# NaN-ignoring maximum over rows: the last key pass of 25 narrow tiles waits for two key buffers at once

## The chip, the cores and the metric

The kernel runs on one core of a Trainium2 chip. Four queues do its work: SyncE (SP) issues the loads and stores, ScalarE (ACT), GpSimd (POOL) and VectorE (DVE) compute; TensorE is not used. Each engine takes its instructions in the order in which they were written, and the engines wait for each other by semaphores that instructions count up. The metric is the time of one execution on the device, in microseconds (us).

## What is computed

```
x: (32, 2048, 2048) float32, a tenth of it NaN
out = nanmax(x, axis=-1)          # (32, 2048) float32
```

65,536 rows of 2048 numbers (536.87 MB) are read once; the maximum of each row without its NaNs is written (0.26 MB). There is next to no reuse, and three passes over the data have to be made while it streams through.

## The kernel before

[...] ScalarE reads them as signed integers and makes a 16-bit *key* (Prelu with a scale of -1, a bias and a steep negative slope: numbers keep their order, NaN patterns go to the far end). A *write-back* then turns the key into the upper half of the float again (times -1, plus TOP), where a NaN has become a very negative number. VectorE reduces the floats by maximum. At the end `find` turns the maxima of rows with nothing but NaNs into NaN.

The rows are spread over 128 partitions and cut into 69 tiles (TILES, numbered from 0), each held by one of three rooms of SBUF. A tile is given as loads, chunks and reductions in units of Q = 512 elements per partition: for each chunk the sizes of the key passes and the sizes of the write-backs. A write-back given as a plain number is POOL's; `(n, w)` is ScalarE's, put off until w more key passes have been issued; `(n, -1)` is VectorE's. Tile 55 is

```
([28], [([8], [(2, 1), 6]), ([8], [8]), ([12], [(3, 1), 9])], [16, 12])
```

one load of 28 Q, chunks of 8, 8 and 12 Q (key passes of 4096, 4096 and 6144 elements); of the first chunk ScalarE writes back 2 Q after the next pass, POOL 6 Q; two reductions of 16 and 12 Q.

Tiles 1 to 35 are wide (32 Q) and keep their keys in place. From tile 38 on (PLAIN) the tiles are narrow, 28 Q and then smaller parts, and the keys go to one of three key buffers of 12 Q, taken in turn. A chunk is put behind the one before it if it still fits; otherwise the next buffer is opened, and the first key pass into it waits until all write-backs out of it are done. `kfree[k]` holds, for each engine, the last write-back out of buffer k; `freed` turns this into waits.

A room is free for a new load when VectorE has made the last reduction of its tile; so the load of tile n + 3 is issued by SP (L495) when VectorE ends tile n. 

The order of the work on each engine is the order of the program's text: for each key pass the pass itself (`act`, L299), then ScalarE's write-backs that are due (`write`, L299), POOL's (L309), then the reductions whose data is written (L316). `Order.needed` leaves out a wait that is implied by one made before on that engine. Of several waits of one instruction the last is attached to it, the others become instructions of their own ahead of it (`engine.wait_ge`, L183).

Where one reduction needs exactly one write-back of ScalarE and one of POOL, `joints` gives the two a *pair* semaphore of their own in place of the engines' counts; whoever waits for the pair waits for both. In `write`, each write-back is entered into `kfree` with the count that the engine's next ordinary instruction will have; in `freed` that count replaces the pair for ScalarE, if it has been given out by then (L408 and the lines after):

```
for back, then, e in uses:
    if back == "act" and order.count["act"] >= then:
        e = ("act", then)
    if back != "pool" or e[0] == "pool" or all(v < then for v in counts):
        deps.append(e)
```

The place of the change is where a buffer is opened (L515):

```
elif used + fresh.get(step, 0) > KEYS:
    key = (key + 1) % NKEYS
    used = 0
    ...
    kold = freed(key, (key + 1) % NKEYS) if number in EARLY and at + c == end else freed(key)
```

`fresh` is the size of a chunk at its first pass; `at + c == end` holds for the last pass of a tile.

Of the kernel before, what the change touches and what calls it, by code (L numbers as in the profile page):

```python
# [91 lines left out]

LANES = 14

EARLY = ()

# [102 lines left out]
def kernel(  # L201
# [91 lines left out]
    with tc.tile_critical() as section:  # L293
# [108 lines left out]
        def freed(*ks):  # L402

            uses = [(back, then, e) for k in ks for back, ((_, then), e) in kfree[k].items()]
            counts = [e[1] for _, _, e in uses if e[0] == "pool"]
            deps = []
# [5 lines that stand above are left out]
            return deps  # L412
# [50 lines left out]
        for number, (loads, chunks, reds) in enumerate(TILES):  # L463
# [44 lines left out]
            for step, c in enumerate(keys):  # L508
# [6 lines left out]
                elif used + fresh.get(step, 0) > KEYS:  # L515
# [3 lines left out]
                    assert all(q[2] != key for v in half.values() for q in v)  # L519
                    kold = freed(key, (key + 1) % NKEYS) if number in EARLY and at + c == end else freed(key)  # L520
                    kfree[key] = {}
# [120 lines left out]
```

## Time and profile before

| | before |
|---|---|
| median of 3 runs | 1252.22 us (1252.11 to 1252.24) |
| the profiled execution | 1252.06 us |
| its span in the profile | 1250.3 us |
| VectorE busy | 1164.8 us (93%) |
| ScalarE busy | 1151.3 us (92%) |
| POOL busy | 1060.2 us (85%) |
| DMA | 537.21 MB, mean 430 GB/s |

The span runs from the first instruction of the program to the end of the last; the execution's time has a little around it. In the rows, a line number such as L299 is that of the helper which records the operation, so most of ScalarE's work has one line, key passes and write-backs alike: `kt<-xt` or `xt<-xt` from uint16<-int16 is a key pass (`xt<-xt` because two of the three key buffers lie in the big tensor), int16<-uint16 is a write-back. A row of the timeline gives start, duration, engine, line, operation, names, shapes and count; in brackets stands how long the engine was idle before it and who ended that. Rows of neighbouring instructions without a break are merged, with their count behind the x. Two instructions of one engine that follow each other closely overlap a little in the records.

### The profile page before, as it was taken

To read this page: it belongs to the slowest core of one execution; us is meant where nothing else is said; L and a number is where in the kernel's file an instruction comes from. 1 tells how busy PE (TensorE), PEld (TensorE's weight loads), DVE (VectorE), ACT (ScalarE), POOL (GpSimd) and SP (SyncE) were. 2 spreads that over 40 slices of the span, in tenths; PEclk is the share of its full clock that TensorE was granted. 3 is DMA by queue.
4 is the path that set the end of the run, shared out by engine and by line. 5 is a ranking of instruction groups with operands and counts; after the bars stand their busy time and mean duration, and the time that the engine had idled before them with its cause. 6 is when DMAs were issued, how large, how long until landed. Compare 5 with 4: busy or idle time off the path is not lost.

```text
span 1250.3 us, 1057 instructions
## 1 busy us (share of the span) xinstructions
DVE 1164.8 (93%) x252; ACT 1151.3 (92%) x294; POOL 1060.2 (85%) x253
## 2 busy tenths in 40 slices
DVE  0799999999999999999999998988889989999999
ACT  3999999999999999999999999898888789999998
POOL 0888788887988888888899998977999887999988
DMA  9999999999999999999999999999999999999997
GB/s 411 428 436 436 436 436 436 436 437 434 436 436 432 432 432 428 434 430 434 434 431 438 433 439 440 433 427 431 440 428 440 426 439 431 431 430 428 432 427 309
DMA packets 17240, 537.21 MB, mean 430 GB/s; under 512 B 2640, under 2 KB 2640, under 8 KB 5712
## 3 DMA queue, kind: packets, MB, share of 16 engines
q1 hardware_dynamic: 17232, 537.14, 99.5%
q14 instruction: 8, 0.07, 0.0%
HBM read 536.87 MB, written 0.26 MB: 430 GB/s over the span
## 4 chain that ended last, share of the span: by engine, by line
DMA 38%; DVE 25%; ACT 23%; POOL 14%; issue 1%; SPq 0%; ACTq 0%
DMA xt<-in_x_dram 38%; DVE acc L316 24%; ACT xt L299 21%; POOL xt L309 14%; ACT kt L299 2%; SPq L495 0%; SPq L286 0%; DVE acc L323 0%; SPq L637 0%; ACTq L183 0%; SPq L293 0%
## 5 line engine op out<-in xcount | busy, mean ns | idle before, releaser
L316 DVE TENSOR_REDUCE acc<-xt 128x3 f32<-128x6144 f32 (+3 forms) x219 | 1114.6, 5135 | 64.2 <-POOL xt L309 56.7
L309 POOL TENSOR_SCALAR xt<-xt 128x3584 int16<-128x3584 uint16 (+9 forms) x204 | 926.3, 4541 | 162.8 <-ACT xt L299 152.9
L299 ACT ACTIVATE xt<-xt 128x6144 uint16<-128x6144 int16 (+12 forms) x236 | 1006.3, 4361 | 62.8 <-DMA xt<-in_x_dram 61.9
L309 POOL TENSOR_SCALAR xt<-kt 128x4096 int16<-128x4096 uint16 (+10 forms) x34 | 128.8, 3789 | 21.2 <-ACT kt L299 19.7
L299 ACT ACTIVATE kt<-xt 128x4096 uint16<-128x4096 int16 (+10 forms) x42 | 118.9, 2852 | 29.7 <-DMA xt<-in_x_dram 29.4
L316 DVE TENSOR_SCALAR xt<-xt 128x2560 int16<-128x2560 uint16 x32 | 52.6, 1644 | 19.0 <-ACT xt L299 19.0
L299 ACT ACTIVATE xt<-kt 128x1536 int16<-128x1536 uint16 (+6 forms) x14 | 29.6, 2112 | 0.2
L331 POOL TENSOR_SCALAR late<-acc 128x112 int32<-128x112 f32 (+1 forms) x5 | 2.8, 558 | 0.4
L299 ACT ACT_TABLE_LOAD x1 | 1.3, 1283 | 1.3 <-SPq L293 1.3
L345 POOL TENSOR_TENSOR acc<-acc,late 128x112 int32<-128x112 int32 (+1 forms) x5 | 2.0, 397 | 0.4
L351 POOL MEMSET scalars<- 128x1 f32 x1 | 0.1, 98 | 0.9 <-SPq L293 0.9
L623 POOL MEMSET const-float32-0.0<- 128x1 f32 x1 | 0.1, 98 | 0.2 <-issue 0.2
L299 ACT ACTIVATE scalars<-scalars 128x1 f32<-128x1 f32 x1 | 0.2, 203 | 0.0
L323 DVE SCALAR_TENSOR_TENSOR acc<-acc 128x7 f32<-128x7 f32 x1 | 0.2, 166 | 0.0
L623 POOL MEMSET const-bfloat16-1.0<- 128x1 bf16 x1 | 0.1, 101 | 0.0
L623 POOL MEMSET const-uint8-127<- 128x1 uint8 x1 | 0.1, 101 | 0.0
L623 POOL MEMSET const-float32-1.0<- 128x1 f32 x1 | 0.1, 98 | 0.0
## 6 DMA issues: line engine op xcount, KB each, us to landing
xt<-in_x_dram SPq DMA_DIRECT2D x20, 7168.0 KB, 23.3
xt<-in_x_dram SPq DMA_DIRECT2D x5, 2304.0 KB, 25.6
xt<-in_x_dram SPq DMA_DIRECT2D x2, 5632.0 KB, 19.6
xt<-in_x_dram SPq DMA_DIRECT2D x3, 3584.0 KB, 25.0
xt<-in_x_dram SPq DMA_DIRECT2D x2, 4352.0 KB, 17.3
xt<-in_x_dram SPq DMA_DIRECT2D x2, 4096.0 KB, 19.7
xt<-in_x_dram SPq DMA_DIRECT2D x1, 7680.0 KB, 24.2
xt<-in_x_dram SPq DMA_DIRECT2D x9, 768.0 KB, 25.3
```

The costliest lines, as they stand in the source:

```text
L299: lambda: nc.scalar.activation(**kw),
L309: lambda: nc.gpsimd.tensor_scalar(**kw),
L316: return order.add("dve", nc.vector, lambda: do(**kw), deps)
L323: lambda: engine.scalar_tensor_tensor(out=acc, in0=acc, scalar=0.0, in1=acc, op0=ALU.mult, op1=ALU.add),
L331: lambda: engine.tensor_scalar(out=none, in0=acc, scalar1=LEAST, scalar2=float(0x00400000), op0=ALU.is_lt, op1=ALU.mult,),
L345: lambda: engine.tensor_tensor(out=bits, in0=bits, in1=none, op=ALU.add),
L351: e_top = order.add("pool", nc.gpsimd, lambda: nc.gpsimd.memset(top, EDGE), [])
L623: nc = _bacc.Bacc("TRN2", target_bir_lowering=False, num_devices=1)
```

## The change

The tuple EARLY, empty before, names 25 tiles. In these, if the last key pass opens a buffer, it waits for the write-backs out of this buffer and out of the next one as well, which the next tile's first pass will open. A wait made there needn't be made again by that later pass, so ScalarE's queue holds 16 wait instructions fewer. Loads, passes, write-backs, reductions, their sizes and their order are the same.

```
-EARLY = ()
+EARLY = (38, 39, 40, 41, 42, 43, 44, 45, 46, 47, 48, 50, 51, 52, 53, 54, 55, 56, 62, 63, 64, 65, 66, 67, 68)
```

## The prediction

> **What bounds the kernel now.** I read the page first, then busy time by stretch, then the chain of waits backwards from the end, and last the timeline of the stretch where the chain leaves the DMA queue. The page:
>
> ```profile
> span 1250.3 us, 1057 instructions
> DVE 1164.8 (93%) x252; ACT 1151.3 (92%) x294; POOL 1060.2 (85%) x253
> q1 hardware_dynamic: 17232, 537.14, 99.5%
> xt<-in_x_dram SPq DMA_DIRECT2D x20, 7168.0 KB, 23.3
> ```
>
> The loads fill 99.5% of the DMA engines' time, so up to the last landing nothing in the middle can cost anything unless the queue runs dry. A full narrow load (7168 KB, 7.34 MB) needs 17.0 us at the page's mean of 430 GB/s and lands 23.3 us after its issue: it is issued some 6 us before its turn. That is the first cover. But the end does not have it. Busy time by stretch (us; VectorE, ScalarE, POOL):
>
> ```profile
> 860.00:960.00 100.00, 88.94 (x16) 85.22 (x24) 91.83 (x19) 1.00 1.00 432
> 1030.00:1074.00 44.00, 41.33 (x8) 42.08 (x13) 36.10 (x9) 1.00 1.00 432
> 1074.00:1167.00 93.00, 92.90 (x20) 88.67 (x29) 88.10 (x25) 1.00 1.00 431
> 1167.00:1248.00 81.00, 80.96 (x32) 77.53 (x57) 72.34 (x36) 1.00 0.94 394
> ```
>
> Up to 1030 every engine has some 10% of room. From 1074 VectorE has 0.1 us of room in 93, and none after. The chain of waits says the same from its other end (start, us, what; pieces from 1030 on):
>
> ```profile
> 1032.08 23.38 DMA xt<-in_x_dram
> ...
> 1098.11 5.92 POOL xt L309
> ...
> 1104.05 21.67 DVE acc L316 x4
> ...
> 1164.35 2.48 POOL xt L309
> ...
> 1166.85 80.96 DVE acc L316 x31
> ```
>
> The last 81 us are 31 reductions without a break, then the last fold of `acc` and its store. So two things bound the time: loads until about 1030, and from there VectorE, which never gets back what it loses. What delays VectorE before 1030 is free as long as the queue is covered; after 1030 it goes to the end almost whole.
>
> **The change part by part.** *Where it acts.* `freed(key, next)` is asked only where the last pass of a tile opens a new key buffer (L515). In tiles 38, 39, 42, 62, 66, 67 and 68 the last pass is put into the buffer already open, by the sizes in TILES: seven of the 25 are not touched. In tile 51 the next buffer's write-back isn't recorded yet when it is asked, so nothing is added there. Seventeen are left: 40, 41, 43 to 48, 50, 52 to 56, 63 to 65.
>
> *What it removes.* The first pass of the next tile waits for its load and, before, for the write-backs of its buffer by an instruction of its own (L183). These go: 16. The chain shows one such wait of ScalarE where it did lie on the path:
>
> ```profile
> 957.49 0.02 issue
> 957.51 0.02 ACTq L183
> 957.53 0.04 issue
> ```
>
> It costs 0.06 us there, between the end of POOL's work (before 957.49) and the start of the pass (957.57). The 16 removed ones stand ahead of a pass that waits for its load; the write-back came earlier, so they are over while ScalarE idles or still runs the pass before. I take 0; at 0.06 each the other end is 16 x 0.06 = 1.0 us gained.
>
> A rule speaks for more. The Trainium skill (Advanced Engine Details and Errata, Network/Comms) gives 50 to 100 ns for a sequencer's reading of a semaphore; by it 16 waits would be an estimated 0.8 to 1.6 us. The one row above agrees with its lower end.
>
> *What it adds, before 1030.* A pass of ScalarE now waits for the POOL write-back of the chunk before the one just written. The largest cases are tiles 45 and 46 (start, us, engine, shapes, idle before):
>
> ```profile
> 857.88 6.48 POOL L309 TENSOR_SCALAR xt<-xt 128x5632 int16<-128x5632 uint16 x1 [5.45 <-ACT xt L299]
> 861.85 3.59 ACT L299 ACTIVATE kt<-xt 128x4096 uint16<-128x4096 int16 x1
> 869.37 9.68 ACT L299 ACTIVATE xt<-xt 128x6144 uint16<-128x6144 int16 x2 [3.94 <-DMA xt<-in_x_dram]
> 874.78 7.06 POOL L309 TENSOR_SCALAR xt<-xt 128x6144 int16<-128x6144 uint16 x1 [0.74 <-ACT xt L299]
> 878.96 2.75 ACT L299 ACTIVATE kt<-xt 128x3072 uint16<-128x3072 int16 x1
> 951.51 13.02 DVE L316 TENSOR_REDUCE acc<-xt 128x3 f32<-128x6144 f32 x2 [1.59 <-POOL xt L309]
> ```
>
> Tile 45: the pass at 861.85 needs the write-back that ends at 857.88 + 6.48 = 864.36, so it starts 2.5 later; ScalarE then idles 3.94 for the next load, and the lag is gone. Tile 46: the pass at 878.96 waits for 874.78 + 7.06 = 881.84, 2.9 later. This lag reaches POOL and VectorE, about 1.9 us, and tile 48's own early wait takes it up once more; but VectorE idles again by 951.51 for a POOL pass that follows a later load, so it ends there. Tiles 41, 43, 44, 48, 50, 52, 53 and 54 have 0.1 to 1.0 us by the same sum, each hidden by ScalarE's idle time for loads, which is
>
> ```profile
> ACT kt L299 <- DMA xt<-in_x_dram: 26.1, 9, 5.0
> ```
>
> 26.1 us in nine waits between 835 and 1034 (total, times, longest). Two us off the six by which a load is issued ahead leaves the queue full. Sum before 1030: 0.
>
> *What it adds in tile 55.* Its three passes have 4096, 4096 and 6144 elements:
>
> ```profile
> 1021.61 3.62 ACT L299 ACTIVATE kt<-xt 128x4096 uint16<-128x4096 int16 x1 [1.28 <-DMA xt<-in_x_dram]
> 1025.31 3.63 POOL L309 TENSOR_SCALAR xt<-kt 128x3072 int16<-128x3072 uint16 x1 [1.53 <-ACT kt L299]
> 1028.64 1.33 ACT L299 ACTIVATE xt<-kt 128x1024 int16<-128x1024 uint16 x1
> 1029.02 4.76 POOL L309 TENSOR_SCALAR xt<-xt 128x4096 int16<-128x4096 uint16 x1
> 1029.84 5.30 ACT L299 ACTIVATE xt<-xt 128x6144 uint16<-128x6144 int16 x1
> 1033.81 15.16 DVE L316 TENSOR_REDUCE acc<-xt 128x4 f32<-128x8192 f32 x2 [1.75 <-POOL xt L309]
> 1035.22 5.34 POOL L309 TENSOR_SCALAR xt<-xt 128x4608 int16<-128x4608 uint16 x1 [1.44 <-ACT xt L299]
> 1036.11 4.47 ACT L299 ACTIVATE kt<-xt 128x5120 uint16<-128x5120 int16 x1 [0.97 <-DMA xt<-in_x_dram]
> 1040.49 14.14 ACT L299 ACTIVATE xt<-xt 128x1536 int16<-128x1536 uint16 x5
> 1040.66 5.90 POOL L309 TENSOR_SCALAR xt<-kt 128x5120 int16<-128x5120 uint16 x1
> 1046.64 3.04 POOL L309 TENSOR_SCALAR xt<-xt 128x2560 int16<-128x2560 uint16 x1
> 1049.00 0.80 SPq L495 DMA_DIRECT2D xt<-in_x_dram  x2
> 1049.72 23.80 DVE L316 TENSOR_REDUCE acc<-xt 128x4 f32<-128x8192 f32 x4 [0.75 <-POOL xt L309]
> 1055.48 3.62 ACT L299 ACTIVATE kt<-xt 128x4096 uint16<-128x4096 int16 x1 [0.85 <-DMA xt<-in_x_dram]
> 1073.69 174.11 DVE L316 TENSOR_REDUCE acc<-xt 128x3 f32<-128x6144 f32 x50 [0.17 <-POOL xt L309]
> ```
>
> The first chunk's buffer is the next one. POOL writes its 3072 back by 1028.94, ScalarE its 1024 by 1029.97. That ScalarE part shares a pair semaphore with POOL's 4096 of the *second* chunk, because one reduction needs both (`joints`). `freed` would put ScalarE's own count in place of the pair, but only if a plain ScalarE instruction has been counted since (`order.count["act"] >= then`); the first one to be counted is this very pass. So it waits for the pair, that is for POOL at 1029.02 + 4.76 = 1033.78: a false dependency on the second chunk. A load lets a pass start 0.02 us after it; by that the pass starts at 1033.80, 3.96 late, and ends at 1039.10.
>
> Behind it, on each engine in order:
> - POOL's 4608 needs this pass: 1039.18 (0.08 after it, as 1035.22 after 1035.14) to 1044.52. POOL has had no other work for 1.44 us before; from here it is packed: 5120 from 1044.60 to 1050.50, 2560 from 1050.58 to 1053.62.
> - VectorE's reduction of tile 56, at 1049.72 now, waits for that 2560: 1053.65, so 3.93 late.
> - ScalarE's next pass (1036.11) starts near 1039.0, 2.9 late; it makes up 0.94 at 1055.48, where it waited for a load. Tile 56's own early wait is for POOL's 5120, 1050.50, and its pass comes at 1051.5: nothing more.
>
> VectorE has next to no idle time left to make it up: 0.25 at 1073.69 (0.17 idle and 0.08 by which reductions otherwise overlap), and 0.1 each at 1104.05 and 1166.85, where it only just waited for POOL, and a little more in the rest: about 0.5. So 3.93 - 0.5 = 3.4 us reach the end.
>
> *The queue.* Tile 55's room comes free at 1049.0 now and near 1051.9 then (its second reduction waits for ScalarE's delayed write-back). The load before lands at 1032.08 + 23.38 = 1055.46, so 3.5 us remain, and after the next, 3.9 late, about as much. What a load needs ahead is shown at the start, where nothing is queued:
>
> ```profile
> 0.74 0.37 SPq L286 DMA_DIRECT2D xt<-in_x_dram  x1
> 5.62 2.47 ACT L299 ACTIVATE xt<-xt 128x2048 uint16<-128x2048 int16 x1 [2.78 <-DMA xt<-in_x_dram]
> ```
>
> 1.05 MB took 4.86 us to 5.60, of which 2.44 is transfer at 430 GB/s: 2.4 us. With 3.5 the queue stays full. Tiles 63 to 65 wait for POOL passes that are over by then. Sum: +3.4, all from tile 55.
>
> The profiled execution took 1252.06 us (span 1250.3 and 1.8 around it), 0.16 under the median of 1252.22. So 1255.5 against its own time, 1255.6 against the median. A change of 0.2%, 2.5 us, is about what can be told from none.
>
> **The rivals.**
> 1. *Not slower: tile 55 waits for its own buffer alone.* If ScalarE's part counts as done by queue order, the pass needs only POOL's 3072, over at 1028.94, before 1029.84. The trace speaks for it in tiles 40 and 63 to 65, where the early wait is met; against it stands the count, one short. It decides at a count of one more. Time: 1252.2.
> 2. *Faster: fewer instructions.* It takes rival 1 as well, and the waits on the path: 1252.2 - 1.0 = 1251.3, still within 0.2%. ScalarE's 92% and its unbroken passes speak for it, the waits for loads against. By the page of the Trainium skill named above it would be an estimated 1250.6.
> 3. *Slower by more: nothing is made up.* All 3.96 stays, and tile 56's early wait bites too, because POOL is packed and its 5120 ends only 1.0 before the pass that now waits for it. 1256.2 to 1257.2. The packed POOL speaks for it; the delay of ScalarE by the same cause speaks against.
>
> **How the numbers follow.** Forecast 0.80, rival 1 0.10, rival 2 0.03, rival 3 0.07. The forecast's own ends: 3.4 with 1.0 given back by the removed waits is 2.4 (1254.6); with nothing made up it is 3.96 (1256.2). Reaching a little below and into rival 3, 1254.0 to 1256.8 leaves out rivals 1 and 2 and part of 3, under 2 in 10. Slower by over 0.2%: 0.86 (forecast and rival 3, less the forecast's lowest end); within: 0.12 (rivals 1 and 2, mostly, and that end); faster: 0.02, since even 1.0 us is too little.
>
> **What would show it.** Right: in tile 55 the 6144 pass starts within 0.1 us of the end of POOL's 4096, near 1033.8; VectorE's idle time before tile 56's reduction grows to over 4 us; 31 or more unbroken reductions end near 1251.2; passes up to 1029 start as now, but for tiles 45 to 48. Wrong in step: the pass at 1029.84 unmoved (rival 1), VectorE's lag shrinking in 1074 to 1248 (idle time that I took for none), or loads landing later than now (a dry queue). The forecast fails most simply if POOL's pass in tile 55 isn't what the pair waits for.

## The result and the profile after

| | before | after |
|---|---|---|
| median | 1252.13 us (1251.91 to 1252.24, 9 runs) | 1255.47 us (1255.28 to 1255.92, 9 runs) |
| profiled execution | 1252.06 us | 1255.28 us |
| span | 1250.3 us | 1253.5 us |

The ratio is 1.0027, with a 95% interval of 1.0017 to 1.0038: slower by 3.3 us. The page of the changed kernel:

```profile
span 1253.5 us, 1042 instructions
DVE 1164.8 (93%) x252; ACT 1152.5 (92%) x294; POOL 1065.2 (85%) x253
q1 hardware_dynamic: 17232, 537.14, 99.3%
```

15 instructions fewer stand in the records, VectorE is as busy as before, and the loads move the same 537.14 MB, which fill a slightly smaller share of a longer span: no more work, and 3.2 us more time. POOL's 5 us more are no part of it: its write-backs of 6144 took 7.33 us on average instead of 7.21, in the wide tiles, where both kernels are the same, and a kernel below that is as fast as the one before had 1055.4 us in all.

Busy time by stretch after (us; VectorE, ScalarE, POOL) shows where the time went:

```profile
860.00:960.00 100.00, 88.94 (x16) 85.31 (x24) 91.87 (x19) 1.00 1.00 432
1030.00:1074.00 44.00, 37.62 (x7) 40.13 (x12) 34.24 (x8) 1.00 1.00 428
1074.00:1167.00 93.00, 93.00 (x19) 89.35 (x30) 88.99 (x25) 1.00 1.00 430
1248.00:1252.00 4.00, 3.18 (x3) 0.00 (x0) 0.00 (x0) 1.00 0.04 7
```

Between 1030 and 1074 VectorE does 3.7 us less than before (41.33 then); between 860 and 960 it does as much as it did. From 1074 on it has no gap at all, and what it lacks stands behind 1248. The chain of waits of the changed kernel has the cause in one piece (start, us, what):

```profile
1028.91 4.75 POOL xt L309
1033.66 0.02 issue
1033.68 5.33 ACT xt L299
1039.01 0.07 issue
1039.09 5.34 POOL xt L309
1044.42 0.08 issue
1044.50 5.90 POOL xt L309
1050.40 0.08 issue
1050.48 3.05 POOL xt L309
1053.53 0.02 issue
1053.56 197.47 DVE acc L316 x54
```

This is tile 55's last pass waiting for the write-back of its second chunk, then POOL, then VectorE, which from there runs 54 reductions without a break to 1251.03. The chain of before left VectorE for a load at 1126.11 and came back at 1166.85; this one doesn't leave it any more. The timeline of the same place:

```profile
1033.68 5.32 ACT L299 ACTIVATE xt<-xt 128x6144 uint16<-128x6144 int16 x1 [3.81 <-POOL xt L309]
1033.68 8.69 DVE L316 TENSOR_REDUCE acc<-xt 128x4 f32<-128x8192 f32 x1 [1.74 <-POOL xt L309]
1045.41 6.55 DVE L316 TENSOR_REDUCE acc<-xt 128x3 f32<-128x6144 f32 x1 [3.04 <-ACT xt L299]
1053.56 30.26 DVE L316 TENSOR_REDUCE acc<-xt 128x4 f32<-128x8192 f32 x5 [1.60 <-POOL xt L309]
1057.48 3.59 ACT L299 ACTIVATE kt<-xt 128x4096 uint16<-128x4096 int16 x1
```

ScalarE, which had no gap here, stands still for 3.81 us. VectorE stands still for 3.04 and 1.60 us before the next two reductions, where it had 0.75 in all.

### The profile page after: what moved, and what is told of

Read it like the earlier page. It is cut to its first block, busy times and chain, and to the rows that moved or that the text cites. A ratio compares the mean times of both kernels' runs of the same rounds, so it can differ in the third digit from the quotient of the medians.

```text
span 1253.5 us, 1042 instructions
## 1 busy us (share of the span) xinstructions
DVE 1164.8 (93%) x252; ACT 1152.5 (92%) x294; POOL 1065.2 (85%) x253
## 3 DMA queue, kind: packets, MB, share of 16 engines
q1 hardware_dynamic: 17232, 537.14, 99.3%
## 4 chain that ended last, share of the span: by engine, by line
DMA 33%; DVE 30%; ACT 22%; POOL 14%; issue 0%; SPq 0%
DMA xt<-in_x_dram 33%; DVE acc L316 30%; ACT xt L299 21%; POOL xt L309 14%; ACT kt L299 2%; SPq L286 0%; SPq L495 0%; DVE acc L323 0%; SPq L637 0%; SPq L293 0%
```

## The experiments

Each kernel ran 11 times, in four groups: the first four rows of the table, the next four, the next three, and the last. In each group the kernel before ran beside them on the same chip; its medians were 1252.46, 1252.04, 1252.59 and 1252.36. Its executions spread over 1.1 to 1.7 us within a group (1251.87 to 1253.55 in the third), so where the interval holds 1, the medians alone don't tell a kernel from the one before.

| kernel | median, us | range | ratio to before, 95% interval |
|---|---|---|---|
| only tile 55 | 1255.39 | 1255.27 to 1255.66 | 1.0023 (1.0014 to 1.0032) |
| all but tile 55 | 1252.29 | 1252.12 to 1253.30 | 0.9999 (0.9990 to 1.0008) |
| all, tile 55 without the pair | 1252.62 | 1252.00 to 1253.92 | 1.0002 (0.9993 to 1.0011) |
| only tile 49 | 1253.47 | 1253.09 to 1253.94 | 1.0007 (0.9998 to 1.0016) |
| only tile 60 | 1253.35 | 1253.22 to 1253.58 | 1.0009 (1.0000 to 1.0018) |
| before, VectorE relieved | 1252.13 | 1251.95 to 1253.04 | 1.0001 (0.9992 to 1.0010) |
| after, VectorE relieved | 1253.68 | 1252.86 to 1254.65 | 1.0012 (1.0003 to 1.0021) |
| before, one more wait per pass | 1252.14 | 1251.96 to 1253.55 | 1.0002 (0.9993 to 1.0011) |
| before, load of tile 58 late | 1252.30 | 1251.96 to 1254.39 | 1.0002 (0.9993 to 1.0011) |
| before, load of tile 59 late | 1252.40 | 1251.84 to 1253.40 | 1.0002 (0.9993 to 1.0011) |
| both late, VectorE relieved | 1252.42 | 1252.00 to 1254.18 | 1.0002 (0.9993 to 1.0010) |
| only tile 55, VectorE relieved | 1253.01 | 1252.12 to 1253.85 | 1.0004 (0.9995 to 1.0013) |

### One tile makes it all, by the pair

Three kernels divide the change. Tile 55 alone:

```
-EARLY = ()
+EARLY = (55,)
```

> EARLY holds tile 55 alone. My theory: tile 55's early wait is the whole effect, so 1255.5 (+3.4 over before), with VectorE unbroken from near 1053.6 to the end. Rival, that the small delays of the other sixteen tiles or the missing wait instructions add up to it: near 1252.2, or clearly under 1255.5.

1255.39: the whole loss, with one tile of 25. All but tile 55:

```
-EARLY = ()
+EARLY = (38, ..., 53, 54, 56, 62, ..., 68)
```

> The change without tile 55. My theory: the same as before, 1252.2 within 0.3, although ScalarE has some fourteen wait instructions fewer and tiles 45 and 46 start a pass 2.5 and 2.9 us late. Rival, that the delays add up: over 1253. Rival, that the missing waits are worth something: up to 1.0 us under before.

1252.29, not to be told from before. The delays of the other tiles are there: its timeline around 860 to 890 has ScalarE waiting for POOL where it waited for nothing before, and a shorter wait for the load behind it.

```profile
864.39 3.62 ACT L299 ACTIVATE kt<-xt 128x4096 uint16<-128x4096 int16 x1 [2.41 <-POOL xt L309]
869.39 9.68 ACT L299 ACTIVATE xt<-xt 128x6144 uint16<-128x6144 int16 x2 [1.38 <-DMA xt<-in_x_dram]
881.87 2.77 ACT L299 ACTIVATE kt<-xt 128x3072 uint16<-128x3072 int16 x1 [2.79 <-POOL xt L309]
```

At 869.39 the pass starts as before (869.37), and the wait for its load went from 3.94 to 1.38 us: 2.5 us late, 2.5 us taken up. The third takes only the pair out of tile 55's early wait; tile 56 waits for the rest itself, as before:

```
 kold = freed(key, (key + 1) % NKEYS) if number in EARLY and at + c == end else freed(key)
+if number == 55:
+    kold = [e for e in kold if e[0] != "pair55_2"]
```

> The change, but tile 55's last pass doesn't wait for the pair semaphore, only for the other write-backs of the next buffer (tile 56's first pass waits for the pair's two halves as before the change). My theory, that the false dependency on the second chunk's write-back is the whole cost: 1252.2, the pass of 6144 starting near 1029.8 again. Rival, that an early wait in this place costs by itself: over 1254.

1252.62, again not to be told from before, and the pass is back in its place:

```profile
1029.82 5.30 ACT L299 ACTIVATE xt<-xt 128x6144 uint16<-128x6144 int16 x1
```

So the early wait costs nothing that shows in tile 55 either, as long as it is for POOL's write-back out of the next buffer. What costs is one semaphore that stands for two write-backs, one of them of another buffer.

### Where a delay falls, and how much it is

```
-EARLY = ()
+EARLY = (49,)
```

> EARLY holds tile 49 alone, which the change leaves out. By the trace of before its last pass (927.98) would then wait for the POOL pass that ends at 932.55: 4.6 us late, more than in tile 55. My theory, that a delay before 1030 is taken up by the waits for loads: 1252.2 within 0.3, VectorE back on time by about 1008. Rival, that the length of the delay decides and not its place: +3 us or more, 1255 to 1256.5.

1253.47 for 1252.46: a delay of 4.6 us, the longest of all, and about 1.0 of it reached the end. The interval just holds 1, but of the 33 executions of the kernel before beside it only three took as long as the shortest of these (1253.09), and the trace has the cause. So place decides more than length, but zero was wrong. Its timeline of VectorE shows it nearly back by 1009 (1008.22 before):

```profile
943.08 10.88 DVE L316 TENSOR_REDUCE acc<-xt 128x4 f32<-128x8192 f32 x2 [3.94 <-POOL xt L309]
969.26 38.91 DVE L316 TENSOR_REDUCE acc<-xt 128x4 f32<-128x8192 f32 x7 [1.34 <-ACT xt L299]
1008.94 6.55 DVE L316 TENSOR_REDUCE acc<-xt 128x3 f32<-128x6144 f32 x1 [0.77 <-POOL xt L309]
```

What didn't come back is in ScalarE's waits for loads:

```profile
971.52 3.19 ACT L299 ACTIVATE kt<-xt 128x3584 uint16<-128x3584 int16 x1 [2.29 <-DMA xt<-in_x_dram]
1005.70 3.62 ACT L299 ACTIVATE kt<-xt 128x4096 uint16<-128x4096 int16 x1 [4.89 <-DMA xt<-in_x_dram]
1022.66 3.62 ACT L299 ACTIVATE kt<-xt 128x4096 uint16<-128x4096 int16 x1 [1.33 <-DMA xt<-in_x_dram]
```

These passes start as their loads land: 970.87, 1004.71 and 1021.61 before, so 0.65, 0.99 and 1.05 later. Tile 49's room came free 4.0 us late, and the load of tile 52 was issued at 951.79, 2.2 us ahead of the landing at 953.96 of the load before it: the queue ran dry. The mean busy share of the 16 DMA engines in half microseconds from 951, summed from the packets of the trace, is 1.00 throughout before and 0.95, 0.31, 0.39, 0.96 from 951.5 to 953.5 here, 0.7 us lost. The loads of tiles 52 and 53 land 0.65 and 0.70 late; those of tiles 53 to 55 were issued 2 to 3.4 us late too, and from tile 56 on the landings are 1.2 late. None of it is made up later, with the loads filling 99.5% of the DMA engines' time.

```
-EARLY = ()
+EARLY = (60,)
```

> EARLY holds tile 60 alone, which the change leaves out. By the trace of before its last pass (1106.32) would wait for the POOL pass that ends at 1109.44: 3.1 us late. It lies in the stretch where VectorE has no room, but ScalarE waits for a load soon after. Working through the rows as for tile 55: tile 61's first pass comes 1.8 us late, POOL's write-backs of tile 61 likewise, and VectorE, which had 1.2 us in hand there, loses 1.2 us for good: 1253.4. Rival, that any delay in the saturated stretch goes to the end whole: 1255. Rival, that it is taken up: 1252.2.

1253.35 for 1252.04, next to the 1253.4 worked out: 3.3 us of standstill on ScalarE, 1.3 us at the end. Its timeline:

```profile
1109.72 8.41 ACT L299 ACTIVATE xt<-xt 128x6144 uint16<-128x6144 int16 x2 [3.34 <-POOL xt L309]
1126.49 4.42 DVE L316 TENSOR_REDUCE acc<-xt 128x2 f32<-128x4096 f32 x1 [0.56 <-POOL xt L309]
1131.34 10.88 DVE L316 TENSOR_REDUCE acc<-xt 128x2 f32<-128x4096 f32 x2 [0.43 <-POOL xt L309]
1142.47 6.55 DVE L316 TENSOR_REDUCE acc<-xt 128x3 f32<-128x6144 f32 x1 [0.25 <-POOL xt L309]
```

VectorE stops for 0.56, 0.43 and 0.25 us in tiles 61 and 62, where it had no gap, and that is what the end pays. Two things took up the rest. ScalarE had waited 1.26 us for the load of tile 61, so its next pass is only 1.8 us late. And VectorE had some ready work in hand: in the kernel before POOL's write-backs were done 1.2 us ahead of the reduction at 1125.64, 0.6 ahead of the one at 1129.96, and 0.1 ahead of the one at 1140.75. So the stock hid less and less of the lag. The expectation took it as 1.2 throughout, which would leave 0.6 of the 1.8, not the 1.2 that it names; that its time came out is in part luck. Every one of these executions is above all 33 of the kernel before beside them. At tile 56 there was no stock: VectorE waited for POOL there already before the change.

### Is it VectorE that carries the lag?

```
-in_=xt[:, lo:done].bitcast(f32).rearrange("p (c d) -> p c d", c=m),
+in_=xt[:, lo:done].bitcast(f32).rearrange("p (c d) -> p c d", c=m)[:, :, 0 : Q if number == 61 and m == 3 else None],
```

in the kernel before and in the changed one: VectorE has 4.8 us less to do in tile 61, behind the place of the delay. These two kernels, called relieved below, leave out three quarters of each row there.

> The kernel before, its last reduction of tile 61 reading only a quarter of each row (three maxima come from 512 of 2048 numbers), so VectorE has 4.8 us less to do near 1136. My theory: little to gain, since POOL and the loads are close behind: 1251.9 to 1252.2. Rival, that VectorE alone bounds the end: 1247.5.

> The changed kernel with the same reduction cut to a quarter of each row. My theory, that the 3.4 us are a lag which VectorE carries for lack of room: with 4.8 us of room behind tile 55 the lag is made up near 1140, and the time is that of the kernel before with the same cut, 1251.9 to 1252.2. Rival, that the lag sits on POOL, on ScalarE or on the loads as well: still 3 us over it, 1255.

The kernel before gains nothing (1252.13), though VectorE is its last bound: POOL is right behind. The changed one falls from 1255.47 to 1253.68. So the larger part of the lag was VectorE's and could be taken up, but 1.5 us stayed, which the theory did not have. VectorE's timeline of the two, first the kernel before, relieved, then the changed kernel, relieved:

```profile
1073.61 62.36 DVE L316 TENSOR_REDUCE acc<-xt 128x3 f32<-128x6144 f32 x13 [0.17 <-POOL xt L309]
1140.59 100.53 DVE L316 TENSOR_REDUCE acc<-xt 128x3 f32<-128x6144 f32 x34 [4.62 <-POOL xt L309]
```

```profile
1054.13 85.91 DVE L316 TENSOR_REDUCE acc<-xt 128x4 f32<-128x8192 f32 x17 [1.60 <-POOL xt L309]
1142.14 98.32 DVE L316 TENSOR_REDUCE acc<-xt 128x3 f32<-128x6144 f32 x33 [2.10 <-POOL xt L309]
```

With the room VectorE gets ahead of its work in both and waits for POOL (4.62 and 2.10 us), so its own lag is gone; but POOL is 1.6 us later there. It follows ScalarE, and ScalarE the loads: tile 61's first pass, which starts as its load lands, starts at

```profile
1116.00 3.62 ACT L299 ACTIVATE kt<-xt 128x4096 uint16<-128x4096 int16 x1 [1.26 <-DMA xt<-in_x_dram]
```

in the kernel before (1115.93 when relieved), and in the changed kernel and in the changed kernel relieved at

```profile
1116.90 3.62 ACT L299 ACTIVATE kt<-xt 128x4096 uint16<-128x4096 int16 x1 [1.00 <-DMA xt<-in_x_dram]
```

```profile
1117.45 3.62 ACT L299 ACTIVATE kt<-xt 128x4096 uint16<-128x4096 int16 x1 [0.97 <-DMA xt<-in_x_dram]
```

0.9 and 1.45 us later (0.45 of the latter was there already at tile 55). So the loads had a lag as well, hidden behind VectorE's larger one. VectorE's lag alone is enough for the whole loss: with tile 55 alone, not relieved, tile 61's load landed 0.1 us late, and the time was 1255.39 all the same.

### The loads: a thin queue is part of it, not all

The loads of tiles 58 and 59 were issued 3.4 and 4.6 us ahead of the landing before them in the changed kernel (6.5 and 7.5 before). To see what that does by itself, SP got one more wait in the kernel before, for tile 58 in the first kernel, for tile 59 by `{59: [("pool", 174)]}` in the second, and for both in the third, which is relieved as above:

```
+LATE = {58: [("act", 189)]}
-before + lanes[turn],
+before + lanes[turn] + (LATE.get(number, []) if at == 0 else []),
```

> The kernel before, with the load of tile 58 held back by one more wait of SP, for the key pass that ends at 1052.68: it is issued 2.8 us ahead of the landing of the load before it instead of 6.5 (in the changed kernel it was 3.4). Nothing else waits for more. Theory formed on the first runs: with so little ahead some of the 16 DMA engines run dry before others, the landing waits for the last, and all later loads come about 1 us later; VectorE has next to nothing in hand at tile 59, so 0.5 to 1.3 us reach the end: 1252.6 to 1253.5. Theory of the prediction, that 2.4 us ahead are enough: 1252.1 as before.

> The kernel before, with the load of tile 59 held back until the POOL pass that ends at 1068.81: issued 3.55 us ahead, as in the changed kernel. Theory of dry engines: a landing 0 to 0.5 us later, as 3.5 is where it begins: 1252.1 to 1252.6. Theory that 2.4 are enough: 1252.1.

> The kernel before with both loads held back (tile 58 2.8 us ahead, tile 59 3.5) and the last reduction of tile 61 cut to a quarter of each row. No wait for a pair, and VectorE relieved. Theory: it shows what the changed kernel with the same cut showed, 1253.0 to 1253.9, since what was left there was the loads' lag. Theory that what was left there came from VectorE or POOL: 1252.1, as the kernel before with the cut.

1252.30, 1252.40 and 1252.42, for 1252.59 beside them: by the medians my theory of dry engines fell in the first and the third kernel; the second lies where both theories allow it. (Its 3.55 us are about what tile 55 alone leaves ahead of tile 59's load, 3.6; in the changed kernel it was 4.6, as the load before landed late itself.) In the first, the load of tile 58 was issued at 1052.59, later than in the changed kernel, and tile 61's pass started at

```profile
1115.90 3.62 ACT L301 ACTIVATE kt<-xt 128x4096 uint16<-128x4096 int16 x1 [1.26 <-DMA xt<-in_x_dram]
```

on time (this kernel is two lines longer). Yet the queue did run dry there: the share of the DMA engines was 0.87, 0.66 and 0.86 in the half microseconds from 1053.0 to 1054.5. The packets of the trace show where time was lost. Listed by the time about which they start are those over 8 KB that took 0.25 us more than usual for their size (2.42 us for 65,536 bytes), as count and worst excess in us; the last column has by how much each of the two loads added to the lateness of the load before it:

```
                          918      935      1053     1071     added at the landing of tile 58, 59 (us)
before                    0        0        0        0        -
after                     2 0.34   4 0.77   5 0.94   2 0.53   +1.0, 0
tile 55 alone             0        0        12 0.86  3 0.41   0, +0.1
after, relieved           4 0.69   3 1.38   8 0.91   12 0.75  +0.6, +0.4
load of tile 58 late      0        0        10 0.92  0        0, 0
load of tile 59 late      0        0        0        8 0.41   0, 0
both late, relieved       0        0        14 1.05  0        0, 0
tile 55 alone, relieved   0        0        12 0.81  1 0.90   0, +0.6
```

A load that is issued late starts with some slow packets, mostly up to 1 us over the usual time each. Why it lands late with some of them and not with others is seen in its semaphore, which gets 16 counts, the last of them at the landing. Tile 58's counts came from 1063.80 to 1065.73 before, from 1064.75 to 1065.63 with its load late, and from 1064.28 to 1066.63 in the changed kernel. So with its load late the first count came 1 us later and the last one no later: the part that landed last had lost nothing, and the others had time to lose. In the changed kernel the last one was hit. That each count is one DMA engine's is taken here, not shown; the packets' records don't name the engine.

One profiled execution of each kernel is not all of them. Two of the eleven with the load of tile 58 late took 1253.90 and 1254.39, and two with both late 1254.02 and 1254.18; none of the 117 executions of the kernel before took more than 1253.55. (One of the kernel without the pair, whose loads of tiles 50 and 51 are issued late, took 1253.92.) So a late load may cost 1 to 2 us now and then, which the medians don't show.

Tiles 46 and 48 make the loads of tiles 50 and 51 late as well (918 and 935), which only the changed kernel has together with tile 55's. They landed on time in the changed kernel and in the two kernels without tile 55's delay; in the changed kernel relieved, tile 51's came 0.3 late. The last run asked whether it takes both:

```
+EARLY = (55,)
 ... [:, :, 0 : Q if number == 61 and m == 3 else None],
```

> EARLY holds tile 55 alone, and the last reduction of tile 61 is cut to a quarter of each row. What was left of the lag in the changed kernel with this cut (1253.7 against 1252.1) came with later loads. In the trace of the changed kernel some DMA engines lose time at the first packets of loads issued late, in two places: tiles 50 and 51 (issued 1.7 us late after tile 46's and 48's waits) and tiles 58 and 59 (after tile 55's). Theory that both are needed for the landing to come late, since each alone hits engines that are ahead of the last one: 1252.0 to 1252.5, with the loads of tiles 58 on within 0.3 of their times before. Rival, that the late loads of tiles 58 and 59 alone do it: 1253.2 to 1253.9.

1253.01, between the two, and widely spread (1252.12 to 1253.85): neither is shown, and the interval holds 1. In its profile the load of tile 58 landed on time and that of tile 59 by 0.6 us late. What stays open is which of the late loads costs how much and in which executions; the runs show only that with both groups of late loads the relieved kernel is clearly slower (1252.86 to 1254.65, where the kernel before, relieved, has 1251.95 to 1253.04), that with tile 55 alone some executions are, and that without the relief it was hidden. Loads lose time now and then without any of this, too: in the profile of tile 60 alone the load of tile 61 landed 0.7 us late, issued 11 us ahead.

### What a wait instruction costs

```
+if number >= PLAIN:
+    nc.scalar.wait_ge(order.sems["pool"], 1)
 e_key = act(
```

> The kernel before with one more wait instruction on ScalarE ahead of each of the 128 or so key passes from tile 38 on, for a POOL count that was reached at the start. My theory, that such waits are hidden behind the pass before or a wait for a load: within 0.3 of 1252.2. Rival, that each costs what one showed on the chain, 0.06 us, or 0.05 to 0.1 us by the Trainium skill (Advanced Engine Details and Errata, Network/Comms): ScalarE loses 6 to 13 us over the stretch, and 2 us or more reach the end.

1252.14. The page of that kernel:

```profile
span 1250.4 us, 1131 instructions
DVE 1163.9 (93%) x252; ACT 1151.4 (92%) x294; POOL 1055.4 (84%) x253
```

74 instructions more than before (1057) came out of the 130 waits written, and 0.1 us, which is less than the runs can tell. ScalarE's waits for loads, which would have shrunk where it lost time, are as they were (total, times, longest):

```profile
ACT xt L299 <- DMA xt<-in_x_dram: 61.8, 45, 17.1
ACT kt L299 <- DMA xt<-in_x_dram: 29.4, 13, 5.0
```

They were 61.9 and 29.4 us before. The 0.06 us in the prediction's row was paid where ScalarE had stood still for that very wait. By the 50 to 100 ns of the Trainium skill (Advanced Engine Details and Errata, Network/Comms) 74 would be an estimated 3.7 to 7.4 us of ScalarE; here the trace does not agree, as nothing of it shows in the span, nor in ScalarE's waits for loads.

## Why the prediction was right, and where not

- *Where it acts, and the whole sum in tile 55*: right. Alone it costs the full amount, without it nothing that shows is left.
- *The pair's false dependency*: right, by the run that takes only the pair out. The pass started 0.02 us after POOL's second chunk, at 1033.68, where the prediction had 1033.80; everything in this execution is 0.1 us earlier at that point.
- *The way behind it*: right in its times: POOL's three write-backs end at 1044.42, 1050.40 and 1053.53 (1044.52, 1050.50, 1053.62), and ScalarE's pass of tile 57 starts at 1057.48, 2.0 late (2.9 less 0.94). VectorE's idle time was wrong in its place: foreseen as over 4 us before tile 56's reduction, it came as 3.04 before the last reduction of tile 55, which waited for ScalarE's delayed write-back, and 1.60.
- *What is made up*: 0.5 of 3.9 foreseen. VectorE starts at 1053.56 instead of 1049.72, 3.84 late, and ends 3.2 late (1251.03 for 1247.81): 0.6. Total 3.2 in the profiled executions and 3.3 between medians, for 3.4.
- *The delays before 1030 at 0*: right for this change, by the kernel without tile 55. As the rule "before 1030 is free", it was too wide: tile 49's 4.6 us cost 1.0, through the queue.
- *The removed waits at 0*: right, as far as the runs can tell: without tile 55 the change still has most of its waits less, at 1252.29 for 1252.46. The end of 1.0 us gained, which came from one row, speaks of waits that ScalarE stands still for; 74 added waits that were already met moved the median by 0.1.
- *The queue stays full*: wrong in part, without effect on the time. The step was "2.4 us ahead are enough", from one load into an idle machine. With 3.4 us the share of the DMA engines stayed at 0.94 or more from 1053.5 to 1055, but some packets took up to 0.9 us longer, and the profile has later loads 1.0 us late, which is one of the prediction's own signs of a wrong step. That it cost nothing was luck: VectorE's lag of 3.2 hid it. With VectorE relieved, 1.5 us of lag were left between the medians, and in the profiles tile 61's load was 1.5 us late. (The prediction's 17.0 us for 7.34 MB at 430 GB/s are 17.1; nothing hangs on it.)
- Rivals 1 and 2 are out by the same runs. Rival 3 had its mechanism in POOL and tile 56; tile 56's early wait did not bite.

## What to carry to other kernels

A semaphore that stands for two events is a dependency on the later of them: here, moving a wait to an earlier place cost nothing for the event that was meant and 3.3 us for its companion. Price a delay by its place: on an engine that waits for loads it is taken up as long as the next loads are still issued in time (2.5 and 2.9 us were, of 4.6 about 1.0 was not); ahead of an engine without room it goes to the end less that engine's stock of ready work. And where two lags run side by side, the smaller is seen only when the larger is taken away.

## What was not expected of the hardware

- A load issued into a queue with 3.4 us left still had slow first packets (5 to 12 of them in the four profiles that have such a load of tile 58, up to 0.9 us over the usual 1.3 us for 34,816 bytes). Its landing came on time in two of them, 0.6 and 1.0 us late in the others.
- An emptied queue need not cost its landing: 0.3 us of all engines' time were lost at 1053 with the load of tile 58 held back, and the load landed within 0.1 us of its time. Its first count came 1 us later and its last did not.
- 74 more wait instructions on ScalarE, for a count already reached, moved a median of 1252 by 0.1 us.
